# Routing in a two-layer prefix DiT kernel: the second norm's rows scaled early on DVE, one product-sum per tile behind the router, and no GpSimd work in the routing

## The chip, the cores and the metric

The kernel runs on one core of a Trainium2 chip. The metric is device time in microseconds of one execution. The core has TensorE (PE; its weight loads are listed apart as PEld), VectorE (DVE), ScalarE (ACT), GpSimd (POOL) and SyncE (SP), which here mostly issues DMA transfers. Each engine runs its own instructions in a fixed order and waits on semaphores for the others.

## What is computed

Two layers over 768 rows of 1024 (256 of context, 512 latent). Each layer norms, projects, runs three mixers (S5, gated recurrence, retention), merges them, projects with `w_out`, adds the residual, norms again, routes each row to two of 32 experts in four groups, and adds the experts' sum. The part around the change is:

```python
def rmsnorm(x, g):
    xf = x.astype(F32)
    y = xf * lax.rsqrt(jnp.mean(xf * xf, axis=-1, keepdims=True) + EPS)
    return (y * g.astype(F32)).astype(x.dtype)

def modulate(h, shift, scale):
    return h * (1.0 + scale) + shift
...
        xl = xl + mod_l[:, 2] * mix[:, n_ctx:]
        h2_l = modulate(rmsnorm(xl, norm2_g[l]), mod_l[:, 3], mod_l[:, 4]).reshape(B * L, D)
...
def hier_moe(t, w_grp, b_grp, w_exp, b_exp, w_gate, w_up, w_down):
    grp_prob = jax.nn.softmax(tf @ w_grp.astype(F32) + b_grp.astype(F32), axis=-1)
    gp, gi = lax.top_k(grp_prob, 1)
    exp_logits = (tf @ w_exp.astype(F32) + b_exp.astype(F32)).reshape(N, N_GROUPS, EXPERTS_PER_GROUP)
    exp_logits = exp_logits[jnp.arange(N), gi[:, 0]]
    ep, ei = lax.top_k(jax.nn.softmax(exp_logits, axis=-1), TOP_K)
    wts = gp * ep / jnp.sum(ep, axis=-1, keepdims=True)
```

In the second layer only the latent rows go on. The experts then take each row's `h2` by its expert and its rank among that expert's rows.

## The kernel before

Rows are held as `x2`, [128 rows, tile, 1024 columns]. `h2` of a row is x2 * rs * A2 + B2: `rs` is the row's reciprocal root mean square, A2 and B2 are two rows of 1024 per condition (context, latent), spread over the partitions.

`post` (the function printed below) is the stage with the `w_out` projection, the second residual and the routing. It goes through blocks of two tiles (256 rows): three in layer 0 (the context, then the latent rows), two in layer 1. For each of the eight column tiles `dt` of a block:

- `wload` (line 1152) loads 128 columns of `w_out`, casts them to a high part on ACT (line 78) and subtracts for the low part (line 79): all products are three matmuls of high and low parts (`mm3`, lines 85 to 88). Its argument `alt`, here `dt % 3`, picks the kind: 0 is a raw tile `wraw` (one buffer) with the low part on POOL, 1 is two half tiles `adaw` (three buffers) with the low parts on DVE, 2 is a raw tile `wraw2` (two buffers) with the low part on POOL. `wh` and `wl`, the two parts, have two buffers each.
- 24 matmuls make the transposed projection, ACT scales it into `z` (line 410), TensorE transposes it back (416) and DVE adds it to x2 (tile `st`). TensorE also transposes x2 itself (405, into the PSUM tile `S`, two banks), DVE copies that out as `xT` (407), and x and z together make the router's logits (371).
- after tiles 3, 6 and 7 ACT squares the columns that are then final (512, 384 and 128) and sums them for the norm (423).

Then `route` (line 441) does the block's routing. On DVE: `rs` by Newton steps, the logits scaled, the softmax of groups, the first and the second expert by maxima and one-hot products (the names `rf..`, `ro`, `rem`, `re`, `rM`), some 35 small operations of two tiles at once; `rMs` (525) is the sum of the two one-hot rows. TensorE makes ranks from it by products with a triangle and with ones (531 to 535, a tile `S`); DVE reads the rank, adds it to the running count `cnt` and makes `code` (547), the row's place for the gather.

Beside that chain `route` makes `h2` and its low part: the odd tile of the block by one pass on ACT (482) and three on POOL (483, 484, split), the even tile on DVE behind `rMs` (539, +B2, split), each with the high cast on ACT, and the low part goes to DRAM (`hl`). The columns are reordered on the way (`pm`, `kq`: a read with a stride).

In the last block of a layer, `gather_first` (called at its tile 6) puts steps of the first expert gathers between: it makes one-hot tiles from `code` (tiles `wraw`, `wh`), multiplies them with `h2` (728) and its low part (729), and the expert stage follows. That stage streams the expert weights in units of 2 MB, which SyncE issues at line 265, into tiles (`u`, `m`) that share space with `post`'s.

A Tile scheduler orders each engine's instructions from the dependences, the pools' buffers and a few explicit ties: `issue_after(x)` holds what is written in it behind instruction x.

Of the kernel before, what the change touches and what calls it, by code (L numbers as in the profile page):

```python
# [21 lines left out]
D = 1024  # L22
# [36 lines left out]
class B:  # L59
# [261 lines left out]
    def post(self, l, M):  # L321
# [4 lines left out]
        with self.pool(f"po{l}") as p:  # L326
# [33 lines left out]
            for lo in range(i0, NT, n):  # L360
# [3 lines left out]
                X, Z = [], []  # L364

# [7 lines left out]
                for dt in range(KD):  # L373
                    wh, wl = self.wload(wp, d["w_out"][l, dt], dt % 3, p)
# [4 lines left out]
                    if dt == 4 and lo in (i0, 2):  # L379
                        for nm, ch in (("B2", 0), ("A2", 1)):  # L380
                            rows[nm] = t = p.tile([128, D], F32, name=nm)
                            self.mrow(t, l, ch, c)
# [36 lines left out]
                    if dt in (3, 6, 7):  # L419
                        q = (3, 6, 7).index(dt)  # L420
                        w = slice((0, 512, 896)[q], 128 * dt + 128)
                        for i in range(n):
                            nc.scalar.activation(self.h2[:, lo - i0 + i, w], x2[:, lo + i, w], AF.Square, accum_out=ss[:, i, q:q + 1])
                logits(0, 0)
                self.route(lo, n, p, pp, rows, lt, R[c][1], ss, hook)
# [15 lines left out]
    def route(self, lo, n, p, pp, rows, lt, rb, ss, hook):  # L441
# [28 lines left out]

        pm = lambda a: a.rearrange("p (q k) -> p k q", k=KD)
# [3 lines left out]

        def h2(i):
            t = p.tile([128, D], F32, name="wraw2", bufs=2) if not hook or i % 2 == 0 else self.wp.tile([128, D], F32, name="wraw")
            return t.rearrange("p (k q) -> p k q", k=KD), pm(self.x2[:, lo + i, :]), t, self.h2[:, lo - i0 + i, :D], self.lows(lo - i0 + i)

        for i in range(1, n, 2):  # L480
            t, x, t1, hi, lw = h2(i)
            nc.scalar.activation(t, x, AF.Copy, scale=rs[:, i:i + 1])
            nc.gpsimd.tensor_tensor(t, t, pm(rows["A2"]), ALU.mult)
            nc.gpsimd.tensor_tensor(t, t, pm(rows["B2"]), ALU.add)
            self.split(hi, lw, t1, nc.gpsimd)
            nc.sync.dma_start(self.hl[lo - i0 + i], self.r(lw))
# [47 lines left out]
        for j in range(n):  # L534
            nc.tensor.matmul(ps[:, 128:160], ones, Ms[:, j], start=j == 0, stop=j == n - 1)
        with self.tc.issue_after(both.ins):
            for i in range(0, n, 2):
                t, x, t1, hi, lw = h2(i)
# [1530 lines left out]
```

## Time and profile before

| | us |
|---|---|
| median of 3 runs | 2812.4 (2806.97 to 2812.46) |
| the profiled execution | 2813.25 |
| its span | 2811.4 |
| `post`, layer 0 / layer 1, read from the trace | 888 to 1061 / 2185 to 2302 |
| PE, DVE, ACT, POOL busy in the span | 88%, 49%, 24%, 25% |
| mean granted TensorE clock | 0.944 |

How to read it: 1.85 us lie outside the span. The shares are means over stages with different limits: mixers, `post` and experts. In a row of a timeline the first number is the start in us from the span's start, the second the duration; a group with a count, such as x2, is several instructions in a row, and the brackets say how long the engine had been idle and what ended that. The number behind L is the line in the kernel, and where a helper does an operation it is the helper's line: L1301 is a DVE tensor_tensor of any kind, L78 and L79 are the high cast and the low part of a split.

### The profile page before, as it was taken

To read this page: it belongs to the slowest core of one execution; us is meant where nothing else is said; L and a number is where in the kernel's file an instruction comes from. 1 tells how busy PE (TensorE), PEld (TensorE's weight loads), DVE (VectorE), ACT (ScalarE), POOL (GpSimd) and SP (SyncE) were. 2 spreads that over 40 slices of the span, in tenths; PEclk is the share of its full clock that TensorE was granted. 3 is DMA by queue.
4 is the path that set the end of the run, shared out by engine and by line. 5 is a ranking of instruction groups with operands and counts; after the bars stand their busy time and mean duration, and the time that the engine had idled before them with its cause. 6 is when DMAs were issued, how large, how long until landed. Compare 5 with 4: busy or idle time off the path is not lost. (4 is left out here: it accounts for less than half of the span.)

```text
span 2811.4 us, 39254 instructions
## 1 busy us (share of the span) xinstructions
PE 2477.0 (88%) x15674; PEld 1678.3 (60%) x15674; DVE 1374.0 (49%) x3210; ACT 664.9 (24%) x1322; POOL 695.8 (25%) x503
## 2 busy tenths in 40 slices
PE   4879999999999869999999599988999879999896
PEld 2657777777888644444444377777777654443342
DVE  8985467576566672122212436777564651111112
ACT  3332321222323431111111333222223421111111
POOL 3552332322323330000001424423224320000002
PEclk8989999999999879999999799899999889999998
DMA  5465443444257429999999533122228649999998
GB/s 210 171 207 179 157 155 122 126 141 138 90 194 248 139 86 379 419 422 422 421 420 411 152 98 125 50 70 83 74 92 286 214 190 420 422 422 422 420 421 272
DMA packets 176160, 667.05 MB, mean 237 GB/s; under 512 B 20672, under 2 KB 40800, under 8 KB 157920
## 3 DMA queue, kind: packets, MB, share of 16 engines
q1 hardware_dynamic: 152608, 586.19, 54.5%
q0 software_dynamic: 15072, 54.01, 6.3%
q10 hardware_dynamic: 8288, 24.27, 2.2%
q8 instruction: 124, 2.03, 0.3%
q14 instruction: 68, 0.56, 0.1%
HBM read 605.12 MB, written 61.38 MB: 237 GB/s over the span
## 5 line engine op out<-in xcount | busy, mean ns | idle before, releaser
L87 PE MATMUL mm<-hH,wh 128*128 128x512 f32 (+1 forms) x1408 | 521.9, 371 | 17.5 <-DVEq L905 6.4
L88 PE MATMUL mm<-hL,wh 128*128 128x512 f32 (+1 forms) x1408 | 510.4, 363 | 0.0
L85 PE MATMUL mm<-hH,wl 128*128 128x512 f32 (+1 forms) x1408 | 507.8, 361 | 2.7 <-POOL wl L79 2.7
L79 POOL TENSOR_TENSOR wl<-wraw,wh 128x1024 fp32r<-128x1024 f32 x117 | 317.2, 2713 | 769.3 <-ACT wh L78 683.3
L666 PE MATMUL gu<-u,wl 128*64 128x512 f32 x1664 | 466.4, 603 | 21.1 <-DMA u<-in_moe_wgu_dram 20.8
L87 PEld LDWEIGHTS mm<-hH,wh 128*128 128x128 f32 x1408 | 275.2, 195 | 85.4 <-issue 35.4
L85 PEld LDWEIGHTS mm<-hH,wl 128*128 128x128 f32 x1408 | 274.5, 195 | 47.2 <-issue 5.3
L666 PEld LDWEIGHTS gu<-u,wl 128*64 128x64 f32 x1664 | 153.0, 139 | 247.6 <-issue 214.2
L88 PEld LDWEIGHTS mm<-hL,wh 128*128 128x128 f32 x1408 | 275.5, 196 | 41.4 <-issue 5.4
L1301 DVE TENSOR_TENSOR wraw<-wraw,gu 128x512 f32<-128x512 f32 x64 | 44.0, 687 | 455.5 <-ACT wraw L671 452.2
L685 PE MATMUL ey<-u,wraw 128*64 128x512 f32 x960 | 230.0, 599 | 0.9 <-ACT wraw L679 0.9
L78 ACT ACTIVATE wh<-wraw 128x1024 fp32r<-128x1024 f32 x117 | 123.2, 1057 | 396.6 <-PE mm L88 296.8
L666 PE MATMUL gu<-m,wl 128*64 128x512 f32 x384 | 171.2, 599 | 22.7 <-DMA m<-in_moe_wgu_dram 22.7
L671 ACT ACTIVATE wraw<-gu 128x512 f32<-128x512 f32 x32 | 19.1, 597 | 657.9 <-PE gu L666 657.8
L685 PEld LDWEIGHTS ey<-u,wraw 128*64 128x64 f32 x960 | 71.2, 137 | 136.6 <-issue 134.1
L720 POOL CAST h<-W 128x8 fp32r<-128x8 f32 (+1 forms) x50 | 9.9, 197 | 554.6 <-PE ext L729 265.5
L728 PE MATMUL ext<-h,wh 128*128 128x384 f32 (+1 forms) x450 | 141.7, 327 | 0.0
L79 POOL TENSOR_TENSOR wl<-adaw,wh 128x512 fp32r<-128x512 f32 x58 | 96.4, 1679 | 168.5 <-ACT wh L78 154.6
L1059 PE MATMUL mm<-adaw,sc 128*32 128x256 f32 x768 | 86.8, 427 | 37.2 <-DMA adaw<-in_w_ada_dram 37.2
L666 PEld LDWEIGHTS gu<-m,wl 128*64 128x64 f32 x384 | 51.5, 138 | 108.8 <-issue 69.3
L729 PE MATMUL ext<-m,wh 128*128 128x384 f32 x360 | 110.3, 319 | 0.0
L728 PEld LDWEIGHTS ext<-h,wh 128*128 128x128 f32 x450 | 84.4, 188 | 24.3 <-issue 23.5
(642 smaller groups left out, 4127.7 us busy)
## 6 DMA issues: line engine op xcount, KB each, us to landing
u<-in_moe_wgu_dram SPq DMA_DIRECT2D x97, 2048.0 KB, 21.1
u<-in_moe_wd_dram SPq DMA_DIRECT2D x55, 2048.0 KB, 21.0
m<-in_moe_wgu_dram SPq DMA_DIRECT2D x24, 2048.0 KB, 23.9
adaw<-in_w_ada_dram SPq DMA_DIRECT2D x160, 256.0 KB, 3.5
wraw<-in_w_in_dram POOLq DMA_DIRECT2D x53, 512.0 KB, 4.0
wraw<-in_w_in_dram SPq DMA_DIRECT2D x27, 512.0 KB, 3.5
wraw<-in_w_out_dram SPq DMA_DIRECT2D x25, 512.0 KB, 3.5
adaw<-in_w_in_dram SPq DMA_DIRECT2D x50, 256.0 KB, 2.9
```

Source lines behind the costliest of these rows:

```text
L78: a = self.nc.scalar.activation(hi, src, AF.Copy)
L79: b = (eng or self.nc.vector).tensor_tensor(lo, src, self.r(hi), ALU.subtract)
L85: low = lambda i: nc.tensor.matmul(out, ops[i][1], ops[i][2], start=False, stop=i == len(ops) - 1)
L87: nc.tensor.matmul(out, lh, rh, start=i == 0, stop=False)
L88: nc.tensor.matmul(out, lh, rl, start=False, stop=False)
L666: self.pin(nc.tensor.matmul(ps[s], xT[:, k, s], w[2 * (k // 4) + u][:, k % 4, 512 * i:512 * i + 512], start=k == 0, stop=k == KD - 1))
L671: nc.scalar.activation(hh, gate, AF.Sigmoid)
L685: self.pin(nc.tensor.matmul(ps[s], hT[:, q, s], w[4 + u][:, q, 512 * h:512 * h + 512], start=q == 0, stop=q == 3))
L728: self.pin(self.nc.tensor.matmul(ps[:, :b - a], oh[:, i], self.h2[:, i, a:b], start=first and i == tiles[0], stop=False, skip_group_check= ...
L729: self.pin(self.nc.tensor.matmul(ps[:, :f - a], oh[:, i], self.lows(i)[:, a:f], start=False, stop=last and i == tiles[-1], skip_group_chec ...
L1059: nc.tensor.matmul(ps[32 * g:32 * g + 32, 256 * c:256 * c + 256], self.sc[:, k + q, 2 - 2 * m:34 - 2 * m], W[n][:, q, :], start=m == 0 and ...
L1301: self.nc.vector.tensor_tensor(o, a, b, op)
```

## The change

The rows' product with A2 leaves the routing: after each group of columns is squared, DVE multiplies it by A2 into two tiles `xa`, one per tile of the block. For them `post` uses the two `wraw2` buffers; the weights then alternate between two kinds (`dt % 2`), not three. A2 is loaded at tile 1, B2 at tile 4. In `route` the odd tile's passes on ACT and POOL are gone. Behind `rMs` DVE makes xa * rs + B2 for both tiles, ACT casts them to `h2` with the strided read, and DVE subtracts for both low parts. The one-hot tile of `gather_first` takes the weights' `wraw` buffer.

```diff
@@ -362,6 +362,7 @@
                 lt = pp.tile([128, 512], F32, name="o", bufs=1)
                 ss = p.tile([128, n, 3], F32, name="rss")
                 X, Z = [], []
+                xa = [p.tile([128, D], F32, name="wraw2", bufs=2) for _ in range(n)]
 
                 def logits(x, z):
 
@@ -371,15 +372,15 @@
                             nc.tensor.matmul(lt[r, :N], R[c][0][:, k, :], a, start=k == 0, stop=k == KD - 1)
 
                 for dt in range(KD):
-                    wh, wl = self.wload(wp, d["w_out"][l, dt], dt % 3, p)
+                    wh, wl = self.wload(wp, d["w_out"][l, dt], dt % 2, p)
                     if (lo, dt) == (i0, 2):
                         R[c] = router(c)
                     if (lo, dt) == (0, 6):
                         R[1] = router(1)
-                    if dt == 4 and lo in (i0, 2):
-                        for nm, ch in (("B2", 0), ("A2", 1)):
-                            rows[nm] = t = p.tile([128, D], F32, name=nm)
-                            self.mrow(t, l, ch, c)
+                    if dt in (1, 4) and lo in (i0, 2):
+                        nm, ch = ("A2", 1) if dt == 1 else ("B2", 0)
+                        rows[nm] = t = p.tile([128, D], F32, name=nm)
+                        self.mrow(t, l, ch, c)
                     if (lo, dt) == (i0, 3):
                         for nm, sh in (("tri", [128, 128]), ("iotar", [128, 32]), ("iotae", [128, 32]), ("one", [128, 1])):
                             t = p.tile(sh, F32, name=nm)
@@ -421,8 +422,11 @@
                         w = slice((0, 512, 896)[q], 128 * dt + 128)
                         for i in range(n):
                             nc.scalar.activation(self.h2[:, lo - i0 + i, w], x2[:, lo + i, w], AF.Square, accum_out=ss[:, i, q:q + 1])
+
+                        for i in range(n):
+                            self.tt(xa[i][:, w], x2[:, lo + i, w], rows["A2"][:, w], ALU.mult)
                 logits(0, 0)
-                self.route(lo, n, p, pp, rows, lt, R[c][1], ss, hook)
+                self.route(lo, n, p, pp, xa, rows, lt, R[c][1], ss, hook)
 
             nb = p.tile([1, E_], F32, name="nb")
             self.nblk(nb, self.cnt[:1])
@@ -438,7 +442,7 @@
         nc.vector.tensor_scalar(nb, nb, MAGIC, None, ALU.add)
         nc.vector.tensor_scalar(nb, nb, MAGIC, None, ALU.subtract)
 
-    def route(self, lo, n, p, pp, rows, lt, rb, ss, hook):
+    def route(self, lo, n, p, pp, xa, rows, lt, rb, ss, hook):
 
         nc = self.nc
         i0 = self.t_lo // 128
@@ -467,23 +471,9 @@
             nc.vector.scalar_tensor_tensor(lg[:, i], lx[:, i], rs[:, i:i + 1], rb, ALU.mult, ALU.add)
         if hook:
             next(hook)
-
-        pm = lambda a: a.rearrange("p (q k) -> p k q", k=KD)
         if (lo - i0) % 4 == 0:
             g = self.groups[(lo - i0) // 4]
             self.low.append(self.buf(*g) if self.whole(g) else self.half(g, "a"))
-
-        def h2(i):
-            t = p.tile([128, D], F32, name="wraw2", bufs=2) if not hook or i % 2 == 0 else self.wp.tile([128, D], F32, name="wraw")
-            return t.rearrange("p (k q) -> p k q", k=KD), pm(self.x2[:, lo + i, :]), t, self.h2[:, lo - i0 + i, :D], self.lows(lo - i0 + i)
-
-        for i in range(1, n, 2):
-            t, x, t1, hi, lw = h2(i)
-            nc.scalar.activation(t, x, AF.Copy, scale=rs[:, i:i + 1])
-            nc.gpsimd.tensor_tensor(t, t, pm(rows["A2"]), ALU.mult)
-            nc.gpsimd.tensor_tensor(t, t, pm(rows["B2"]), ALU.add)
-            self.split(hi, lw, t1, nc.gpsimd)
-            nc.sync.dma_start(self.hl[lo - i0 + i], self.r(lw))
         bc = lambda a, m: a[:, :, None].to_broadcast([128, n, m])
         gl = lg[:, :, :4]
         gm, ge, gs, gp = f("gm"), f("ge", 4), f("gs"), f("gp")
@@ -533,12 +523,16 @@
                 nc.tensor.matmul(o, ones, Ms[:, j], start=False, stop=j == i - 1)
         for j in range(n):
             nc.tensor.matmul(ps[:, 128:160], ones, Ms[:, j], start=j == 0, stop=j == n - 1)
+
         with self.tc.issue_after(both.ins):
-            for i in range(0, n, 2):
-                t, x, t1, hi, lw = h2(i)
-                nc.vector.scalar_tensor_tensor(t, x, rs[:, i:i + 1], pm(rows["A2"]), ALU.mult, ALU.mult)
-                self.tt(t, t, pm(rows["B2"]), ALU.add)
-                self.split(hi, lw, t1)
+            for i in range(n):
+                nc.vector.scalar_tensor_tensor(xa[i], xa[i], rs[:, i:i + 1], rows["B2"], ALU.mult, ALU.add)
+            for i in range(n):
+                h, lw = self.h2[:, lo - i0 + i, :D], self.lows(lo - i0 + i)
+                pm = lambda a: a.rearrange("p (q k) -> p k q", k=KD)
+                kq = lambda a: a.rearrange("p (k q) -> p k q", k=KD)
+                nc.scalar.activation(kq(h), pm(xa[i]), AF.Copy)
+                self.tt(kq(lw), pm(xa[i]), kq(self.r(h)), ALU.subtract)
                 nc.sync.dma_start(self.hl[lo - i0 + i], self.r(lw))
         rk = f("rk", 32)
         self.tt(rk, ps[:, :32 * n].rearrange("p (i e) -> p i e", e=32), self.cnt[:, None, :].to_broadcast([128, n, 32]), ALU.add)
@@ -773,7 +767,7 @@
 
         nt = self.h2.shape[1]
         a, b = range(nt - 2), range(nt - 2, nt)
-        oh = p.tile([128, KD, 128], F32R, name="wraw2", bufs=2)
+        oh = self.wp.tile([128, KD, 128], F32R, name="wraw")
         self.onehot(0, oh, a)
         self.beside(0, a)
         yield
```

How instructions stand on the engines, in the routing of layer 0's first block. First DVE, from the last one-hot products to the code. `S` is the rank, `m` a low part, `wraw` the tile in which a row is scaled. Before:

```order
L1301 TENSOR_TENSOR rM_9365<-rog,ro_9363 128x32 x2
L525 TENSOR_TENSOR rMs<-rM_9364,rM_9365 128x64
L539 SCALAR_TENSOR_TENSOR wraw_9398<-x_8851,rrs,A_9100 128x1024
L1301 TENSOR_TENSOR rrk<-S,cnt 128x64
L1301 TENSOR_TENSOR wraw_9398<-wraw_9398,B_9098 128x1024
L1301 TENSOR_TENSOR cnt<-S,cnt 128x32
L547 SCALAR_TENSOR_TENSOR code<-rrk,rMs 128x64
L553 TENSOR_SCALAR rm_9366<-rw_9368 128x2
L407 COPY xT<-S 128x256
L554 RECIPROCAL rm_9366<-rm_9366 128x2
L1301 TENSOR_TENSOR x_8851<-x_8851,st 128x2x128
L79 TENSOR_TENSOR m_9335<-wraw_9398,h_8861 128x1024
```

After:

```order
L515 TENSOR_TENSOR rMs<-rM_9369,rM_9370 128x64
L529 SCALAR_TENSOR_TENSOR wraw_8886<-wraw_8886,rrs,B_9104 128x1024
L529 SCALAR_TENSOR_TENSOR wraw_8887<-wraw_8887,rrs,B_9104 128x1024
L1295 TENSOR_TENSOR m_9347<-wraw_8886,h_8861 128x1024
L1295 TENSOR_TENSOR rrk<-S,cnt 128x64
L1295 TENSOR_TENSOR m_9347<-wraw_8887,h_8861 128x1024
L1295 TENSOR_TENSOR cnt<-S,cnt 128x32
L541 SCALAR_TENSOR_TENSOR code<-rrk,rMs 128x64
```

Both low parts now stand between `rMs` and the code; before, the one low part that DVE made stood behind it.

TensorE in the same place, where 531 to 535 (after: 521 to 525) are the rank, 405 (406) the transposes of x2 and 87 and 88 the projection of the next block. Before:

```order
L416 MATMUL st<-ident,z 128x128 x2
L531 MATMUL S<-rMs,tri 128x32 x2
L533 MATMUL S<-rMs,one 128x32
L535 MATMUL S<-rMs,one 128x32 x2
L405 MATMUL S<-ident,x_8851 128x128 x6
L371 MATMUL o<-xT,wA 36x256
L405 MATMUL S<-ident,x_8851 128x128 x2
L371 MATMUL o<-xT,wA 36x256 x2
L87 MATMUL mm<-m1a,wh 128x256
```

After:

```order
L87 MATMUL mm<-m1a,wh 128x256
L521 MATMUL S<-rMs,tri 128x32 x2
L523 MATMUL S<-rMs,one 128x32
L525 MATMUL S<-rMs,one 128x32 x2
L406 MATMUL S<-ident,x_8851 128x128 x2
L88 MATMUL mm<-m1b,wh 128x256
```

Seven matmuls of the third weight tile now stand ahead of the rank, and 36 projection matmuls between the first two transposes and the next two; before, eight transposes and three logits products stood ahead of the first of them.

POOL in the same block. Before:

```order
L79 TENSOR_TENSOR wl<-wraw,wh 128x1024 x2
L483 TENSOR_TENSOR wraw_9336<-wraw_9336,A_9100 128x1024
L484 TENSOR_TENSOR wraw_9336<-wraw_9336,B_9098 128x1024
L79 TENSOR_TENSOR m_9335<-wraw_9336,h_8861 128x1024
L720 CAST h_8861<-W 128x2x2
```

After:

```order
L233 CAST h_8861<-zero 128x6x8
L79 TENSOR_TENSOR wl<-wraw,wh 128x1024 x5
L714 CAST h_8861<-W 128x2x2
L715 TENSOR_TENSOR h_8861<-W,h_8861 128x2x2
L79 TENSOR_TENSOR wl<-wraw,wh 128x1024 x5
```

The three passes of the odd tile are gone; splits of weights and two small operations are left.

## Rows read from the trace of the kernel before

**Rows 1.** Chain that ended last, late in layer 1: start, duration, what.
```profile
2418.31 32.32 DMA u<-in_moe_wgu_dram
```

**Rows 2.** Stretches: length, busy PE, PEld, DVE, ACT, POOL (instructions), clock, DMA share, GB/s.
```profile
900.00:910.00 10.00, 10.00 (x78) 8.99 (x78) 2.56 (x5) 3.29 (x8) 3.39 (x2) 1.00 1.06 374
940.00:950.00 10.00, 3.45 (x15) 2.93 (x16) 9.43 (x24) 2.02 (x3) 2.73 (x2) 0.50 0.29 105
2310.00:2320.00 10.00, 10.00 (x54) 5.65 (x51) 1.38 (x2) 2.87 (x4) 0.00 (x0) 1.00 0.99 421
```

**Rows 3.** Timeline of SyncE's issues behind the last block, layers 0 and 1.
```profile
1061.10 1.32 SPq L265 DMA_DIRECT2D u<-in_moe_wd_dram  x2
...
2301.27 8.98 SPq L265 DMA_DIRECT2D u<-in_moe_wgu_dram  x4
```

**Rows 4.** Waits of TensorE in `post`, layer 0: total us, times, longest.
```profile
PE S L531 <- DVE rMs L525: 19.9, 2, 11.3
PE S L531 <- issue: 7.7, 1, 7.7
```

**Rows 5.** Timeline of DVE: block 0 of layer 0, then its last block.
```profile
919.40 1.29 DVE L79 TENSOR_TENSOR wl<-adaw,wh 128x512 fp32r<-128x512 f32 x2
...
934.72 2.77 DVE L1301 TENSOR_TENSOR rf1e<-rf1e,iotar 128x16 f32<-128x16 f32 x1
...
941.57 2.36 DVE L1301 TENSOR_TENSOR ro<-iotar,rf2i 128x16 f32<-128x16 f32 x1
...
944.29 0.22 DVE L525 TENSOR_TENSOR rMs<-rM,rM 128x64 f32<-128x64 f32 x1
...
947.10 1.99 DVE L1301 TENSOR_TENSOR wraw<-wraw,B 128x1024 f32<-128x1024 f32 x1
...
949.11 0.22 DVE L547 SCALAR_TENSOR_TENSOR code<-rrk,rMs 128x64 f32<-128x64 f32 x1
...
1037.84 0.16 DVE L551 TENSOR_REDUCE rgs<-rge 128x2 f32<-128x8 f32 x1 [0.97 <-ACT rge L492]
...
1048.09 0.23 DVE L525 TENSOR_TENSOR rMs<-rM,rM 128x64 f32<-128x64 f32 x1
```

**Rows 6.** Timeline of POOL, block 0 of layer 0.
```profile
934.61 2.85 POOL L483 TENSOR_TENSOR wraw<-wraw,A 128x1024 f32<-128x1024 f32 x1 [6.32 <-ACT wraw L482]
...
941.56 2.34 POOL L79 TENSOR_TENSOR m<-wraw,h 128x1024 fp32r<-128x1024 f32 x1 [1.17 <-ACT h L78]
```

**Rows 7.** Single lines: ns min/median/max; ACT pass, DVE product, DVE product-sum (final norm).
```profile
L482 ACT ACTIVATE wraw<-x,rrs x5: 2130/2274/2402, 932.1 to 2277.8; 128x1024 f32<-128x1024 f32 x5
...
L539 DVE SCALAR_TENSOR_TENSOR wraw<-x,rrs,A x5: 2089/2096/2110, 944.4 to 2290.5; 128x1024 f32<-128x1024 f32 x5
...
L1013 DVE SCALAR_TENSOR_TENSOR fnx<-x,fnr,gf x2: 1283/1284/1285, 2800.0 to 2803.4; 128x1024 f32<-128x1024 f32 x2
```

**Rows 8.** Groups by line in 888:1062: busy, mean ns, idle before; ACT, then POOL.
```profile
L78 ACT ACTIVATE wh<-wraw 128x1024 fp32r<-128x1024 f32 x14 | 14.3, 1048 | 8.0 <-PE mm L88 4.2 <-DMA wraw<-in_w_out_dram 2.0 <-issue 1.7
...
L79 POOL TENSOR_TENSOR wl<-wraw,wh 128x1024 fp32r<-128x1024 f32 x14 | 33.2, 2381 | 44.7 <-ACT wh L78 39.5 <-PE S L405 5.2
```

**Rows 9.** Timeline of TensorE: block 0, then the gather behind the last block.
```profile
954.37 0.58 PE L87 MATMUL mm<-m1a,wh 128*128 128x256 f32 x1
...
1054.09 0.69 PE L728 MATMUL mm<-h,wraw 128*128 128x384 f32 x1 [3.31 <-ACT h L78]
1055.86 0.69 PE L729 MATMUL mm<-m1a,wraw 128*128 128x384 f32 x1 [1.08 <-DVE m1a L79]
```

**Rows 10.** DMA issues in `post`, layer 0: times, KB each, median us to landing.
```profile
wraw<-in_w_out_dram SPq DMA_DIRECT2D x14, 512.0 KB, 3.5
...
m<-in_moe_wgu_dram SPq DMA_DIRECT2D x1, 2048.0 KB, 7.5
```

**Rows 11.** Timeline of ACT, block 1 of layer 0, two weight tiles apart.
```profile
958.43 0.46 ACT L410 ACTIVATE z<-mm,mc 128x256 f32<-128x256 f32 x1
...
966.16 0.46 ACT L410 ACTIVATE z<-mm,mc 128x256 f32<-128x256 f32 x1
```

## The prediction

> **What bounds the kernel now.** I read the views in this order: the chain that ended last, the table by stretches, TensorE's waits, and then DVE and GpSimd (POOL) side by side around the routing.
>
> The chain shows that late in layer 1 the expert stage waits about 32 us at a time for its weights [rows 1], and there the DMA engines are full (share 0.99, 421 GB/s) [rows 2]. So the expert stage ends a fixed number of bytes after its stream began. SyncE issues the first units behind the routing of the last block at 1061.10 us in layer 0 and 2301.27 in layer 1 [rows 3]; just before that, the DMA engines have little to do. Whatever `post`, the stage with the routing, gains is therefore passed on, 1:1, to the end. `post` has five blocks of two tiles: three in layer 0, two in layer 1.
>
> Inside a block TensorE is full (10.00 of 10 us in 900:910, 78 matmuls, 0.128 us each), and around a routing it is not: 3.45 of 10 us in 940:950, at a granted clock of 0.50, the lower level, while DVE is at 9.43 [rows 2]; the other blocks read alike. The waits name why: the rank matmuls (line 531) wait for `rMs`, 7.7 us in block 0, 8.7 and 11.3 in the other two of layer 0 (19.9 together) [rows 4]. The row that says "issue" is the same wait with no releaser found. The routing's DVE chain is what ends last.
>
> Why is the chain long? Most of its operations take 0.15 to 0.3 us, but some take over 2. At 934.72 the operation on `rf1e` (16 columns) takes 2.77 us, at 941.57 one on `ro` 2.36 [rows 5]. Beside them stand POOL's routing operations: 934.61 for 2.85 us, which ends at 937.46, and 941.56 for 2.34, which ends at 943.90 [rows 6]. Each long DVE operation ends when POOL's does: a DVE operation with two inputs in SBUF that starts under a POOL tensor_tensor lasts until that is over. Each block has three such; against 0.17 each undisturbed they cost 7.3 us in block 0, and by the same reading 6.6 to 7.3 in the five blocks.
>
> **The change part by part.**
>
> *POOL leaves the routing.* The three locks disappear: 6.6 to 7.3 us of the chain in every block. With the strided ACT pass (2.13 to 2.40 us [rows 7]) gone from ahead of the group softmax's exponential, DVE's wait for it (0.97 us in layer 0's last block [rows 5], 0.8 to 1.1 in three of the five) goes too. Not all of POOL goes: in the interior blocks (two in layer 0, one in layer 1) the scheduler puts one weight split of 2.38 us [rows 8] in the same stretch. It costs 0, if no two-input operation starts under it, to 2.4; I take 1.2, as it can hold back at most one operation and on average for half its time. The last blocks load no further weights and have none.
>
> *The weight tiles alternate in two kinds in place of three.* POOL splits per block go from five to four, DVE pairs from three to four. A pair is 1.29 us [rows 5], and in two of the three interior blocks it now stands inside the chain, ahead of `rMs`: 0.9 on the mean of the three. Elsewhere DVE is 2.56 of 10 us busy [rows 2] and hides it.
>
> *Multiplying by A2 as columns get final.* Six operations per block over 512, 384 and 128 columns. No row has this operation; the nearest is the 1.29 us for two of 512 columns, scaled by columns: 2 x (0.65 + 0.5 + 0.25) = 2.8 us a block. Four fifths of it lie under TensorE's work of tiles 4 to 7, with DVE three quarters idle [rows 2]; that of the last 128 columns (0.5, and 0.3 of ordering) comes just before the chain. I take 0.6 in interior and 0.3 in last blocks, where the logits' matmuls run beside it; bounds 0 and 2.8.
>
> *Between `rMs` and the code.* Now: one strided product 2.09 us [rows 7], the rank's read, +B2 1.99, count, code at 949.11, 4.8 us after `rMs` at 944.29 [rows 5]. After: two product-sums, contiguous. The nearest row is the final norm's product-sum over 1024 columns, 1.28 [rows 7]; by the strided row it would be 2.09, but nothing is strided now. They end at +1.4 and +2.7. ACT's two copies now read strided, as line 482 does: 2.27 each, from +1.4, so +3.8 and +6.1 (1.05 each if it were the plain cast [rows 8]). DVE's low parts read strided too: 1.99 each, bounds 1.29 and 2.09, the first from +3.8 to +5.8, the second from +6.1 to +8.1; then count and code, at about +8.3. So the code comes 3.5 us later after `rMs` than now. In two of the interior blocks an ACT operation that waits for TensorE (`z`) stands ahead of the copies; there it can be +11.
>
> Who waits for the code? It frees the PSUM bank that the transposes (line 405) need. Before the change, TensorE has those transposes ahead of everything, and its first projection matmul comes at 954.37 [rows 9], 10.1 us after `rMs`. In the new order some 36 projection matmuls stand between rank and transposes, 36 x 0.128 = 4.6 us of work that fills the wait. When the bank comes free at +8.3, some 3 us of transposes and logits (an estimate: what TensorE does between the code at 949.11 and 954.37, at twice the clock) are left: equivalent to +8.3 + 3.0 - 4.6 = +6.7, 3.4 better than now; with +11 it is +9.4, 0.7 better. Over the three: about 1.6 + 0.8 for the stretch that runs at the full clock again = 2.4.
>
> An interior block then gains 7.0 + 0.4 (the exponential, on the mean) - 1.2 - 0.9 - 0.6 + 2.4 = 7.1, held by what TensorE idles (7.7 and 8.7 [rows 4], part of which is not reached); I take 6.7, bounds 3 and 10.
>
> *The last block of each layer.* `rMs` comes 6.9 + 0.8 = 7.7 us earlier. Behind it, now: the gather's first matmul at 1054.09, 6.0 us after `rMs` (1048.09 [rows 5]), and its second at 1055.86, +7.8, which waited for DVE's low part [rows 9]. After: the code at +8.3, the one-hot 0.4 later, matmuls from +8.9 with nothing more to wait for: 1.4 later than now. 7.7 - 1.4 - 0.3 = 6.0, bounds 4.5 and 7.5.
>
> **Sum.** 3 x 6.7 + 2 x 6.0 = 32.1 us. The profiled execution took 2813.25 us (its span 2811.4, and 1.85 around it): 2781. The median of the runs shown is 2812.4, 0.9 less, within the difference of these runs, so nothing is added. By the bounds alone: 3 x 3 + 2 x 4.5 = 18 gives 2795, 3 x 10 + 2 x 7.5 = 45 gives 2768.
>
> **The rivals.**
>
> [...]
>
> *Only the last blocks gain.* DVE is the busy engine around an interior routing, 9.43 of 10 us [rows 2]; what it takes on can eat the 7. Behind `rMs` it had 2.09 + 1.99 + 1.29 = 5.4 us of such work and gets 2 x 1.28 + 2 x 1.99 = 6.5, 1.1 more; with the weight pair 1.3, the A2 products' tail 0.6, the remaining lock at its upper bound 2.4 and the wait for ACT's copies 1.1 that is 6.5. If the work ahead of the bank's wait only moves TensorE's idle time behind it, 12 us remain, of the last blocks: 2801.
>
> *The locks come back in another place.* The A2 products are operations with two SBUF inputs, and four POOL splits of 2.4 us per block run in the same 40 us. If each of the three pairs started under one, it would wait about 2.3: 3 x 2.3 x 5 = 35 us if all were on the path, about the whole gain: 2812. For it: the rows at 934.61 and 934.72. Against: TensorE's work covers DVE there. The Trainium skill, "SBUF — State Buffer", section "Who interferes with whom", says that DVE instructions with two SBUF inputs contend with a GpSimd instruction that reads SBUF, and that issue order decides who blocks. By that rule the locks on the DVE products are possible, but POOL's splits can as well be the ones that wait; the trace agrees with the first half (2.77 us for a 0.17 us operation).
>
> *Slower: one raw buffer sets the pace.* Weight tiles of the first kind now all load into a single buffer, every second tile, where before two more raw buffers took every third. A cycle of it is issue 0.33 + landing 3.5 (median of 14 [rows 10]) + ACT 1.05 + POOL 2.38 [rows 8] = 7.3 us; TensorE takes 7.7 for two tiles (`z` at 958.43 and 966.16, [rows 11]). It fits by 0.4. ACT waits 2.0 us for such a load in `post` already [rows 8]. While other transfers run, landing can be 7.5 us (the unit of the expert stage in `post` [rows 10]); then a cycle is 11.3 and each pair 3.6 late. With three pairs in each of five blocks, 15 x 3.6 = 54 us against the 32 gained: 2835. It decides from a landing of 5.9 us on (32 / 15 = 2.1 per pair). Against it: the DMA engines have slack in most of `post`, and two tiles' splits may run ahead.
>
> **How the numbers follow.** Forecast 2781 (own range 2768 to 2795): 0.53. Larger, 2769: 0.14. Only the last blocks, 2801: 0.15. Locks elsewhere, 2812: 0.09. Raw buffer, 2835: 0.09. The range 2766 to 2806 takes in the first three, about 0.8. A measurement of this kernel tells 0.2%, 5.6 us, from no change. Faster 0.83, same 0.09, slower 0.08.
>
> **What would show it.** Right: in the changed profile no operation of the chain between `rem` and `rMs` takes over 0.5 us in the last blocks and at most one in the others; the rank's wait shrinks to 0 to 3 us in interior blocks; SyncE's stream starts at about 1042 in place of 1061.10 in layer 0 (two interior blocks and a last one: 19.4 us) and 12.7 us sooner after the start of `post` in layer 1; the expert stage's own length is unchanged. Wrong: A2 products of 2 us; long waits of TensorE for `wh` or `wl` in `post`; the code later than +11.

## The result, and the profile after

The changed kernel takes 0.9848 of the time of before (95% interval 0.9825 to 0.9871): 42.7 us less, about 2770 where 2781 was forecast. The median of its four runs is 2762.5 us (2758.2 to 2779.9), against 2812.4; that median by itself lies 3.5 us below the forecast range, the ratio puts the time inside. A second series beside other kernels gave 0.9836 (0.9812 to 0.9861). Direction and mechanism were as forecast, the size a quarter too small.

The page of the profiled execution (2762.2 us): span, busy time by engine, granted clock.

```profile
span 2760.4 us, 39281 instructions
...
PE 2458.6 (89%) x15674; PEld 1671.8 (61%) x15674; DVE 1364.3 (49%) x3255; ACT 664.8 (24%) x1322; POOL 641.2 (23%) x483
...
PEclk8989999999999989999999799898999999999998
```

TensorE's waits in `post` of layer 0 (total us, times, longest):

```profile
PE mm L722 <- DVE rt L1295: 5.9, 1, 5.9
PE S L521 <- DVE rMs L515: 4.8, 2, 3.4
PE S L406 <- DVE cnt L1295: 2.9, 1, 2.9
...
PE S L521 <- issue: 1.9, 1, 1.9
PE mm L87 <- ACT wh L78: 1.2, 1, 1.2
```

The rank (now line 521) waits 6.7 us in the three blocks, where it waited 27.6 [rows 4]; in the interior ones it is 1.9 and 1.4. The last block's gather (now line 722) waits 5.9 us at its first product; before, it waited 3.3 and 1.1 at its first two [rows 9]. The row that names a weight tile (`wh`) is 1.2 us: the single raw buffer holds hardly anything up.

DVE in the first block, from the last `ro` to the code, and in the last block (rows that answer to [rows 5]), then POOL in the first block [rows 6]:

```profile
931.58 0.18 DVE L1295 TENSOR_TENSOR ro<-iotar,rf2i 128x16 f32<-128x16 f32 x1
931.96 2.34 DVE L547 TENSOR_SCALAR rm<-rw 128x2 f32<-128x2 f32 x1 [0.20 <-ACT rw L509]
...
934.53 0.22 DVE L515 TENSOR_TENSOR rMs<-rM,rM 128x64 f32<-128x64 f32 x1
934.67 2.47 DVE L529 SCALAR_TENSOR_TENSOR wraw<-wraw,rrs,B 128x1024 f32<-128x1024 f32 x2
938.18 2.10 DVE L1295 TENSOR_TENSOR m<-wraw,h 128x1024 fp32r<-128x1024 f32 x1 [1.04 <-ACT h L534]
...
942.52 0.24 DVE L541 SCALAR_TENSOR_TENSOR code<-rrk,rMs 128x64 f32<-128x64 f32 x1
...
1017.19 0.23 DVE L515 TENSOR_TENSOR rMs<-rM,rM 128x64 f32<-128x64 f32 x1
...
1024.85 0.22 DVE L541 SCALAR_TENSOR_TENSOR code<-rrk,rMs 128x64 f32<-128x64 f32 x1
```

```profile
931.91 2.37 POOL L79 TENSOR_TENSOR wl<-wraw,wh 128x1024 fp32r<-128x1024 f32 x1 [8.81 <-ACT wh L78]
```

The operation on `ro` that took 2.36 us takes 0.18. One lock is left in this block, under the weight split at 931.91. SyncE's stream of expert weights starts here (answers to [rows 3]):

```profile
1030.52 1.05 SPq L265 DMA_DIRECT2D u<-in_moe_wd_dram  x2
...
2247.61 13.30 SPq L265 DMA_DIRECT2D u<-in_moe_wgu_dram  x4
```

The starts of `rrs` (the scale), `rMs` and `code` and of the first expert product (`gu`) cut each routing into stretches. All in us, from the DVE and TensorE timelines; an interior block runs to the next block's scale. For layer 0's last block the rows are these, first before (`rMs` is in [rows 5]), then after (`rMs` is above):

```profile
1035.17 0.16 DVE L108 SCALAR_TENSOR_TENSOR rrs<-n22t,n22y 128x2 f32<-128x2 f32 x1
...
1061.17 1.41 PE L666 MATMUL gu<-u,wl 128*64 128x512 f32 x4
```

```profile
1012.13 0.16 DVE L108 SCALAR_TENSOR_TENSOR rrs<-n22t,n22y 128x2 f32<-128x2 f32 x1
...
1030.88 7.51 PE L660 MATMUL gu<-u,wl 128*64 128x512 f32 x33 [0.31 <-ACT wl L752]
```

| stretch | before | after | gained |
|---|---|---|---|
| layer 0, block 0: scale to rMs / rMs to next scale | 12.36 / 39.21 | 7.46 / 35.44 | 4.9 + 3.8 |
| layer 0, block 1 | 12.79 / 38.88 | 8.08 / 34.08 | 4.7 + 4.8 |
| layer 0, last: scale to rMs / rMs to gu | 12.92 / 13.08 | 5.06 / 13.69 | 7.9 - 0.6 |
| layer 1, block 0 | 12.36 / 38.87 | 8.20 / 34.37 | 4.2 + 4.5 |
| layer 1, last | 12.76 / 11.99 | 5.07 / 13.56 | 7.7 - 1.6 |

Sum: 40.2 us. The spans of the two profiled executions differ by 51; the other 10.8 lie outside the routings. A second trace of the unedited changed kernel, below, has the same stretches to 1.1 us and a span 11.5 us longer: in it the routings gain 41.6 us and the rest loses 2.1. So what lies outside differs between executions of one kernel, and the gain that stays is that of the routings.

### The profile page after: what moved, and what is told of

Read it like the earlier page. It is cut to its first block, busy times and chain, and to the rows that moved or that the text cites. A ratio compares the mean times of both kernels' runs of the same rounds, so it can differ in the third digit from the quotient of the medians.

```text
span 2760.4 us, 39281 instructions
## 1 busy us (share of the span) xinstructions
PE 2458.6 (89%) x15674; PEld 1671.8 (61%) x15674; DVE 1364.3 (49%) x3255; ACT 664.8 (24%) x1322; POOL 641.2 (23%) x483
## 5 line engine op out<-in xcount | busy, mean ns | idle before, releaser
L79 POOL TENSOR_TENSOR wl<-wraw,wh 128x1024 fp32r<-128x1024 f32 x112 | 302.6, 2702 | 802.6 <-ACT wh L78 705.3
L660 PE MATMUL gu<-u,wl 128*64 128x512 f32 x1664 | 470.1, 606 | 14.1 <-DMA u<-in_moe_wgu_dram 13.4
L87 PEld LDWEIGHTS mm<-hH,wh 128*128 128x128 f32 x1408 | 273.6, 194 | 72.6 <-issue 30.6
L660 PE MATMUL gu<-m,wl 128*64 128x512 f32 x384 | 177.0, 616 | 28.4 <-DMA m<-in_moe_wgu_dram 28.4
L1053 PE MATMUL mm<-adaw,sc 128*32 128x256 f32 x768 | 85.2, 421 | 42.9 <-DMA adaw<-in_w_ada_dram 42.6
## 6 DMA issues: line engine op xcount, KB each, us to landing
u<-in_moe_wd_dram SPq DMA_DIRECT2D x55, 2048.0 KB, 19.4
m<-in_moe_wgu_dram SPq DMA_DIRECT2D x24, 2048.0 KB, 23.9
```

Source lines behind the costliest of these rows:

```text
L79: b = (eng or self.nc.vector).tensor_tensor(lo, src, self.r(hi), ALU.subtract)
L87: nc.tensor.matmul(out, lh, rh, start=i == 0, stop=False)
L660: self.pin(nc.tensor.matmul(ps[s], xT[:, k, s], w[2 * (k // 4) + u][:, k % 4, 512 * i:512 * i + 512], start=k == 0, stop=k == KD - 1))
L1053: nc.tensor.matmul(ps[32 * g:32 * g + 32, 256 * c:256 * c + 256], self.sc[:, k + q, 2 - 2 * m:34 - 2 * m], W[n][:, q, :], start=m == 0 and ...
```

## Experiments

**The locks, put back.** In the changed kernel, POOL gets three products that nothing uses:

```diff
+        for i in range(1, n, 2):
+            t, x = self.h2[:, lo - i0 + i, :D], self.x2[:, lo + i, :]
+            nc.gpsimd.tensor_tensor(t, x, rs[:, i:i + 1].to_broadcast([128, D]), ALU.mult)
+            nc.gpsimd.tensor_tensor(t, x, rows["A2"], ALU.mult)
+            nc.gpsimd.tensor_tensor(t, x, rows["B2"], ALU.mult)
```

> The changed kernel with three POOL products of 1024 columns (both inputs in SBUF) put back behind the second norm's scale in every routing, about 8.5 us of POOL work per block; nothing uses what they write. Theory (POOL's reads hold up DVE's two-input operations): up to three operations of the chain take 2 to 2.9 us again, rMs comes 5 to 7 us later in the last blocks and 3 to 6 in the interior ones, and the kernel is 20 to 30 us slower than the changed one. Rival A (the gain came from the weights' raw buffers and TensorE's order, which stay): only the last blocks lose, 10 to 14 us together. Rival B (POOL never mattered): within 5 us of the changed kernel.

Measured: 0.996 of before (0.9945 to 0.9974), some 31 us slower than the changed kernel. DVE and POOL in its last block of layer 0:

```profile
1030.21 2.06 DVE L471 SCALAR_TENSOR_TENSOR rlg<-rlx,rrs,rb 128x36 f32<-128x36 f32 x2
...
1032.51 2.16 DVE L1300 TENSOR_TENSOR rge<-rlg,rgm 128x8 f32<-128x8 f32 x1
...
1034.78 2.34 DVE L1300 TENSOR_TENSOR rfge<-rfge,iotar 128x8 f32<-128x8 f32 x1
```

```profile
1030.31 1.91 POOL L479 TENSOR_TENSOR h<-x,rrs 128x1024 fp32r<-128x1024 f32 x1 [16.01 <-issue]
1032.30 2.34 POOL L480 TENSOR_TENSOR h<-x,A 128x1024 fp32r<-128x1024 f32 x1
...
1034.76 2.33 POOL L481 TENSOR_TENSOR h<-x,B 128x1024 fp32r<-128x1024 f32 x1
```

Each long DVE operation ends with the POOL operation beside it: 1034.78 + 2.34 and 1034.76 + 2.33. Scale to `rMs` is 10.8 us in the last blocks (5.1 without) and 13.7 to 14.1 in the interior ones. By the stretches the five blocks lose 33 us to the changed kernel, 21.7 of them in the interior blocks, and 29.5 of the 33 ahead of `rMs`. The theory holds, with a loss just above the 20 to 30 us expected; both rivals fall, the first by the interior blocks.

**POOL that only writes.** Same place; one product of 8 columns ties six fills to the scale:

```diff
+            nc.gpsimd.tensor_tensor(t[:, :8], x[:, :8], rs[:, i:i + 1].to_broadcast([128, 8]), ALU.mult)
+            for _ in range(6):
+                nc.gpsimd.memset(self.r(t), 0.0)
```

> As the run before, but POOL only writes: one product of 8 columns and six fills of 1024 columns with zero in every routing; nothing uses what they write. Theory (only a POOL instruction that reads SBUF holds DVE up): the chain's operations stay at 0.15 to 0.3 us but for those under weight splits, and the time is within 4 us of the changed kernel. Rival (any POOL work in that stretch costs): 10 to 25 us slower than it.

Measured: 0.9855 (0.9823 to 0.9888), as the changed kernel. The fills did lie beside the chain, 5.9 us of them in the last block of layer 0; the same two operations as above, `rge` and `rfge`, under the first two:

```profile
1014.48 1.97 POOL L481 MEMSET h<- 128x1024 f32 x2
...
1017.60 2.97 POOL L481 MEMSET h<- 128x1024 f32 x3
```

```profile
1014.76 0.17 DVE L1300 TENSOR_TENSOR rge<-rlg,rgm 128x8 f32<-128x8 f32 x1
...
1015.04 0.17 DVE L1300 TENSOR_TENSOR rfge<-rfge,iotar 128x8 f32<-128x8 f32 x1
```

Scale to `rMs` is 5.09 us there. What holds DVE's two-input operations up is POOL's reading of SBUF, not POOL's being busy. The Trainium skill, "SBUF — State Buffer", section "Who interferes with whom", has this distinction (a GpSimd instruction that reads SBUF, not one that only writes it); the two runs agree with it, 2.16 and 2.34 against 0.17 us.

**The kernel before without POOL in the routing.** The odd tile's loop is dropped and the even tile's runs over all:

```diff
-        for i in range(1, n, 2):
-            t, x, t1, hi, lw = h2(i)
...
-            for i in range(0, n, 2):
+            for i in range(n):
                 t, x, t1, hi, lw = h2(i)
```

> The kernel before, with the odd tile of each block made on the path of the even one (two DVE passes and a DVE low part behind rMs), so that no POOL and no strided ACT pass is left in the routing; weights still in three kinds, A2 not early. Theory (locks in the chain are one part of the gain, the weights' raw buffers the other): rMs comes 6 to 7 us sooner in each block, the code 4 to 5 us later behind it (a second product, +B2, low part), so 1 to 3 us are gained per block: 8 to 15 us against before. Rival (the locks are the whole gain): 25 to 40 us.

Measured: 0.9961 (0.9947 to 0.9976), 11 us gained, some 7 of them in the two last blocks by the stretches. Scale to `rMs` is 5.04 to 5.08 us in all five blocks, but from scale to scale an interior block still takes 49.6 to 50.9 (51.2 to 51.7 before). TensorE shows where the time went:

```profile
943.25 1.40 PE L405 MATMUL S<-ident,x 128*128 128x128 f32 x4 [8.66 <-DVE cnt L1294]
```

```profile
949.39 2.01 ACT L78 ACTIVATE wh<-wraw 128x1024 fp32r<-128x1024 f32 x2 [7.64 <-DMA wraw<-in_w_out_dram]
```

It now stands 8.7 us at the transposes, until the count is read behind both tiles' rows, and has no third weight tile to work on: that tile's raw buffer is one of the two that the rows hold, and its load is issued at 943.46, behind them. The wait only changed its name.

**The kernel before with two kinds of weight tile.**

```diff
-                    wh, wl = self.wload(wp, d["w_out"][l, dt], dt % 3, p)
+                    wh, wl = self.wload(wp, d["w_out"][l, dt], dt % 2, p)
```

> The kernel before with one edit: weight tiles alternate between two kinds, so that the third tile of the next block loads into the weights' own buffer and not into one that the routing's rows hold. Theory (the shared raw buffer kept TensorE without a third weight tile during the routing): TensorE works on the third tile under the chain and behind the rank, its waits at the rank fall from 7 to 9 us to under 5 in the interior blocks, the low clock there shortens, and the kernel gains 10 to 20 us; the last blocks stay. Rival A (as the prediction had it: the kinds alone are worth nothing): within 5 us of before. Rival B (the single raw buffer sets the pace): 5 to 50 us slower than before.

Measured: 0.9973 (0.9956 to 0.9991), 7.6 us gained, under the theory's 10 to 20. The interval, 2.5 to 12 us, does not part the theory from rival A (within 5 us); by the stretches the interior blocks gain 1.0, 3.2 and 2.9 us, so the kinds alone are worth something, and less than expected. Its rank still waits, weights hardly:

```profile
PE S L531 <- DVE rMs L525: 20.4, 2, 11.3
PE S L531 <- issue: 8.6, 1, 8.6
...
PE mm L87 <- ACT wh L78: 2.2, 1, 2.2
```

So the waits at the rank did not shrink as the theory had it: the chain itself grew, from 12.4 and 12.8 us to 14.5 to 15.5 in interior blocks, as the third tile's split on POOL now runs in it and holds one more operation. Behind `rMs` the stretch is 33.0 to 36.1 us in place of 38.9 to 39.2. The rival that the single raw buffer sets the pace falls here too.

**Both edits together.**

> The kernel before with both edits of the two runs before this one: no POOL work in the routing (the odd tile made like the even one) and weights in two kinds; A2 still applied behind rMs. From one scale to the next, a pair of interior blocks took 51.7 us before, 42.2 to 42.9 in the changed kernel, 50.9 with the first edit alone and 48.5 to 50.6 with the second alone. Theory (each alone leaves the other wait standing: without POOL, TensorE stands at the transposes until the code, having no third weight tile; with the tile, the chain is still locked): both together give 43 to 46 us, the last blocks stay near 21.8 from scale to first expert product as in the first edit, and the kernel gains 25 to 35 us against before; what is left to the changed kernel, 8 to 15 us, is A2 applied early. Rival (the two parts add up: 11 + 8): 17 to 22 us gained, interior pairs 47 to 50.

Measured: 0.9911 (0.9885 to 0.9938), 25 us; interior blocks 43.9 to 45.8 us from scale to scale. That is more than 11 + 7.6, as the theory had it, though the interval reaches down to the sum of the two. The traced stretches decide: the interior blocks gain 5.8, 7.8 and 6.2 us, where the two single edits add up to 1.7, 4.1 and 4.5. To the changed kernel some 17 us are left, 13 by the stretches: `rMs` to code is 10.4 us in the last blocks (7.7 there), and 11.4 to 13.2 in interior ones (8.0 to 10.1). The early A2 products and the single product-sum take that off, but not by shorter DVE work alone. In two interior blocks of this run a weight split on POOL starts under DVE's four passes over the rows and lasts past them: it takes 7.62 us (from 983.29) and 8.59 us (from 2205.58) in place of 2.4. Then it holds up DVE's first low part, 3.24 us in place of 1.2, and TensorE waits for it, 2.2 us in layer 0 and 4.1 in layer 1, a wait that the changed kernel does not have. The row of the low part, then TensorE's wait in layer 0:

```profile
988.75 3.24 DVE L79 TENSOR_TENSOR m<-wraw,h 128x1024 fp32r<-128x1024 f32 x1
```

```profile
PE mm L85 <- POOL wl L79: 2.2, 1, 2.2
```

**TensorE kept busy in the last block.** In the changed kernel, behind the rank:

```diff
+        if hook:
+            fill = pp.tile([128, 512], F32, name="S", bufs=2)
+            for _ in range(10):
+                nc.tensor.matmul(fill[:, :256], self.ident, self.x2[:, lo, :256], start=True, stop=True)
```

> The changed kernel with ten products of 256 columns that nothing uses, on TensorE behind the rank of the last block of each layer, where it idles 5.9 us. Theory (the low clock of 13.7 us in each last block follows from that idle time and doubles the time of the gather's twelve products): the granted clock stays at or returns to 1.00 there, the products take 0.28 to 0.35 us in place of 0.41 to 0.53, code to first expert product falls from 6.0 to 4 to 4.5 us, 3 to 5 us for the kernel, which is at the edge of what is measured. Rival (the gather waits for its copies on ACT and DVE, not for TensorE): under 1 us; or the fill overshoots and the gather starts up to 2 us later.

Measured: 0.9861 (0.9838 to 0.9884), no difference from the changed kernel. The table by stretches (PE, PEld, DVE, ACT, POOL, clock, DMA share, GB/s), around the code of layer 0's last block (at 1024.85 and 1029.95), first without the fill, then with it; the second still has some 2 us of the fill in it:

```profile
1024.00:1028.00 4.00, 2.25 (x7) 2.28 (x8) 4.00 (x20) 0.49 (x1) 0.44 (x2) 0.50 0.56 224
```

```profile
1028.00:1032.00 4.00, 3.08 (x16) 2.54 (x16) 4.00 (x13) 0.19 (x1) 0.02 (x1) 1.00 0.65 260
```

The clock did come back, from 0.50 to 1.00, and the products took 0.34 us in place of 0.52; code to first expert product fell from 6.0 to 5.2 us in layer 0 and from 5.9 to 5.3 in layer 1, 0.9 and 0.6 us where 1.5 to 2 were expected. Layer 0's gather got 1.3 us shorter, but its first expert product then waits 0.9 us for a copy on DVE (`sw`), where it had waited 0.3 for one on ACT.

**The code first.** The reads of the rank, the count and the code are written ahead of the casts and low parts.

> The changed kernel with the count and the code written ahead of the casts and low parts, so that the code stands behind one low part and not two. Theory (the bank that the code frees is covered by TensorE's work in interior blocks, and in the last blocks the gather also needs the second low part): rMs to code falls from 7.7 to about 5.9 us, scale to first expert product by 0 to 2, interior pairs by 0 to 1: 0 to 6 us in all. Rival (the code's place is what bounds): 2 us in each of five blocks, 10 us.

Measured: 0.9864 (0.9842 to 0.9886), no gain. `rMs` to code fell to 5.6 us in the last blocks, as expected; code to first expert product grew from 6.0 to 8.0. The gather's one-hot is next on DVE behind the second low part, so it starts at about the same distance from `rMs` as before (7.7 us, 8.0). The rival falls.

**The columns reordered early.** The early A2 products write the columns in the reordered order, B2 is reordered once per condition, and with the code first:

```diff
-                            self.tt(xa[i][:, w], x2[:, lo + i, w], rows["A2"][:, w], ALU.mult)
+                            xq = xa[i].rearrange("p (k q) -> p k q", k=KD)[:, :, w.start // KD:w.stop // KD]
+                            self.tt(xq, pm(x2[:, lo + i, w]), pm(rows["A2"][:, w]), ALU.mult)
...
-                nc.scalar.activation(kq(h), pm(xa[i]), AF.Copy)
-                self.tt(kq(lw), pm(xa[i]), kq(self.r(h)), ALU.subtract)
+                self.split(h, lw, xa[i])
```

> The changed kernel with the reordering of columns moved into the early A2 products (their output strided, B2 reordered once per condition through a buffer that is free then), so that behind rMs the product-sum, ACT's cast and the low part are all contiguous, and with the code ahead of the casts. Theory (what is behind rMs is on the path in the last blocks, what is under the projection is covered): per tile 2.27 becomes 1.05 on ACT and 2.0 becomes 1.25 on DVE, rMs to code falls from 7.7 to 4 to 4.5 us, the second low part ends at +5.5 in place of +8, scale to first expert product falls from 18.7 to 15.5 to 16.5 us, interior pairs by 0 to 3: 5 to 14 us for the kernel against the changed one. Rival (strided products ahead of the chain, some 5.6 us per block in place of 3, delay the scale): the gain is given back, 0 to 5 us slower.

Measured: 0.9813 (0.9798 to 0.9829), median 2753.7 us. Behind `rMs` in the last block:

```profile
1018.87 2.48 DVE L532 SCALAR_TENSOR_TENSOR wraw<-wraw,rrs,B 128x1024 f32<-128x1024 f32 x2
...
1021.40 1.22 DVE L79 TENSOR_TENSOR m1a<-wraw,h 128x1024 fp32r<-128x1024 f32 x1
...
1022.63 0.22 DVE L537 SCALAR_TENSOR_TENSOR code<-rrk,rMs 128x64 f32<-128x64 f32 x1
```

`rMs` to code is 3.9 us (7.7 before this edit), scale to first expert product 15.7 and 16.4 us in the two layers (18.8 and 18.6). The strided products, 1.90 us for two of 384 columns in place of 1.03, are covered for the most part: scale to `rMs` is 8.1 us in block 0 (7.5) and unchanged elsewhere, but in layer 0 TensorE now waits 5.6 us for `xT`, a copy that DVE makes, and the interior blocks take 40.3 to 43.8 us from scale to scale, about what they took.

**Side by side on one chip.** The changed kernel again, the last one again, and the last one with six unused products behind the rank:

> The changed kernel, unedited, as the yardstick of the two runs beside it on the same chip, and a second trace of it. Expected: 0.983 to 0.987 of before, and the same stretches as in its first trace to 0.5 us (interior pairs 42 to 43 us from scale to scale, last blocks 18.6 to 18.8 from scale to first expert product); the stages outside the routing may differ by several us between executions, as the time at the low clock does there.

> The reordered early products with the code first, a second time, beside the changed kernel on the same chip. Theory: 5 to 10 us faster than the changed kernel, most of it in the last blocks (15.7 to 17 us from scale to first expert product). Rival (its gain of the run before was a difference of chips and sessions): within 3 us of it.

> The same with six unused products of 256 columns on TensorE behind the last blocks' rank, where it idles 4.1 us. Theory (the clock is worth only the gather's products, of which a part is covered by their copies): the granted clock is 1.00 at the gather, and 0.5 to 1 us per layer is gained, less than a measurement tells. Rival (the low clock after the idle time costs several us): 4 us or more.

Measured: 0.9836 (0.9812 to 0.9861), 0.9794 (0.9774 to 0.9814) and 0.98 (0.9777 to 0.9823); medians 2764.8, 2755.0 and 2751.7 us. In the traces of the first two, interior blocks take 41.0 to 42.9 against 40.0 to 42.2 us and last blocks 19.0 and 18.4 against 16.4 and 16.4: 8 us of routing. The reordered kernel beats both the kernel before and the changed one by the medians, about 10 us from the latter; the two intervals touch at their ends. What the fill adds cannot be told from nothing by the times. In its trace the clock is back at 1.00 as the gather starts, and the last blocks take 15.3 and 15.9 us, 1.2 and 0.5 less than without it, about the theory's 0.5 to 1. The second trace of the changed kernel keeps the stretches of the first to 0.3 us but for two interior blocks, 0.6 and 1.1 us shorter, where 0.5 was expected.

## Why the prediction was right, and where its sizes were off

- *What bounds.* Right. `post`'s gain passed to the end. Layer 0's stream starts 30.6 us sooner, of which 4.2 had come before `post` began; 26.4 against the 19.4 forecast. In layer 1 it starts 17.5 us sooner after the start of `post`, and the first expert product 13.1 us; 12.7 was forecast. From that product to the end it is 507.4 us, 509.1 before.
- *The size by blocks.* The interior blocks gave 26.8 us where 3 x 6.7 = 20.1 was forecast, the last ones 13.4 where 12.0 was.
- *The locks.* Right, and shown by putting them back (31 of some 42 us go) and by fills that only write (none goes). The last blocks' chain shortened by 7.9 and 7.7 us; 7.7 was forecast. The signs named for it came: between `rem` and `rMs` no operation over 0.5 us in the last blocks and at most one elsewhere, and 1.4 to 1.9 us of wait at the rank in interior blocks.
- *The lock that is left.* Too low: 1.2 us was taken as half of one operation. All three interior blocks have a lock of nearly full length: 2.34 on `rm` in block 0, and in block 1 and in layer 1 the operations on `rlg` take 2.46 and 2.47 us (0.42 undisturbed). The whole chain of an interior block gained 4.2 to 4.9, for which the terms up to `rMs` gave 7.0 + 0.4 - 1.2 - 0.9 = 5.3. The row for block 1:

```profile
970.16 2.46 DVE L471 SCALAR_TENSOR_TENSOR rlg<-rlx,rrs,rb 128x36 f32<-128x36 f32 x2
```

- *Behind `rMs`, interior blocks.* The term that was mis-sized. Forecast 2.4, less 0.6 for the A2 products: 1.8. Measured 3.8 to 4.8. The code came 3.2 to 5.2 us later after `rMs` than before, as forecast (3.5, or 6 with `z` ahead), so the excess is in what TensorE does meanwhile. The prediction had the 36 matmuls that fill the wait, and put 0.8 us a block on the clock without a row for it. The views by stretches, summed in steps of 0.25 us, part the excess. TensorE's busy time in the three interior blocks, in us:

| | before | after |
|---|---|---|
| `rMs` to the next scale | 36.6, 35.1, 34.9 | 34.5, 29.6, 31.8 |
| of that at the low clock (0.50) | 9.1, 8.2, 8.3 | 6.2, 3.4, 6.8 |
| ahead of it, scale to `rMs` | 3.4, 3.9, 3.9 | 4.1, 6.0, 6.2 |

  As an estimate from these, with busy time at 0.50 counted as half lost, the 13.1 us that the three blocks gained are 6.1 of matmul work that left the stretch, 4.6 of clock and 2.4 of idle time. So the clock gave 1.5 us a block where 0.8 was put down. The largest part is the third weight tile's matmuls, which now run under the chain: the order of TensorE's instructions in block 0 shows seven of them ahead of the rank, but the sum counts only the 36 behind it. No run holds the clock fixed, so this split is worked out and not tested.
- *The larger gain.* The measured time, 2770 by the ratio, lies at the figure of the larger gain (2769) and not at the forecast's 2781. The 12 us that it adds to the forecast no run shows by themselves. In neither trace of the changed kernel do all interior routings run at the full clock: over the two `post` stretches (880 to 1075, and 2160 to 2315 us) the time at the low clock fell from 54.6 and 37.5 us to 23.9 and 20.5. The first four rank matmuls take 0.60 us in block 1, at the full clock, where block 0's, at 0.50, take 1.03. By the estimate above the clock gave 4.6 us in the interior blocks, so that the time meets this figure is in part luck.
- *Why the order changed.* The prediction read the order rightly and gave no reason. The two runs of single edits give it: the third weight tile's raw buffer was shared with the routing's rows. Neither that nor the locks was worth much alone (7.6 and 11 us), since each left the other wait standing; together 25.
- *Strided copies, product-sums, A2.* Right: two product-sums 2.47 (forecast 2 x 1.28), ACT's copies 2.14 each on the mean (2.27), low parts 2.0 to 2.2 (1.99), the last products of 128 columns 0.48 (0.5). They were on the path where forecast: taking the strides out, together with the code first, which alone gave nothing, was about 10 us faster by the medians.
- *Last blocks, behind `rMs`.* 0.6 and 1.6 us later, 1.4 forecast.
- *Rivals.* "Only the last blocks gain" fell: interior blocks gave 26.8 of the 40.2 us. "Locks elsewhere" happened and cost nothing that shows: two pairs of A2 products were held, 2.99 us for 512 columns in place of 1.3 (at 901.62) and 1.92 for 384 in place of 1.03 (at 2183.20), both under TensorE's work. "Raw buffer" fell: 1.2 us of waits for `wh` in layer 0. The landing time from which it would decide is 6.0 us by its own terms (7.7 + 2.1 - 0.33 - 1.05 - 2.38), not 5.9.

## What to carry to other kernels

Look for small DVE operations that take ten times their usual time and end with an operation on GpSimd: work moved to GpSimd to relieve DVE is not free where a latency chain of two-input operations runs beside it, and it costs up to its own length per operation that starts under it. It can go the other way too: work on GpSimd that starts under a row of long two-input DVE operations waits for them. When a wait is removed and the time hardly moves, look at what the waiting engine would do next and whether that has its buffers; here two edits, worth 8 and 11 us alone, gave 25 together. A stride that must be paid somewhere is cheapest where the engine is covered by another's work.

## What was not expected of the hardware

A DVE operation with one input was held too: the tensor_scalar on `rm`, 128x2 elements, 2.34 us under a POOL split, where the same operation took 0.17 elsewhere. It was not the only one: in the same trace a tensor_scalar of 128x4 (`rtc`) took 1.95 and 1.97 us under splits, at 994.74 and 2216.22. And it was held by a fill, which only writes: in the run with the fills, `rm` in block 0 took 0.96 us and ended with the fill beside it, the first of two that take 1.97 us together from 935.61.

```profile
935.63 0.96 DVE L552 TENSOR_SCALAR rm<-rw 128x2 f32<-128x2 f32 x1
```

In the other four blocks of that run it took 0.17 to 0.43 us. But for the one queued behind that `rm`, the chain's two-input operations ran beside the fills of 1024 columns, 0.95 to 0.99 us each, at their usual length. No run was made on the one-input form. Not held in the changed kernel were an addition with one input in PSUM, `x<-x,st`, 0.42 us at 901.16 under the split that started at 901.09, and a reduction, `rk`, 0.22 us at 944.68 under the split from 944.47.

The hold goes the other way as well. The weight split at 980.33, which starts under DVE's product-sums, takes 2.63 us in place of 2.37; under the four DVE passes of the run with both edits it takes 7.62 and 8.59.
